# Windowed sums by a scan, conditioning dots placed elsewhere, and weights fetched two ahead, in a two-layer trunk

## The chip, the cores and the metric

One core of a Trainium2 chip runs the whole kernel. Its engines work side by side: TensorE multiplies matrices, VectorE (DVE) and ScalarE (ACT) do elementwise work, GpSimd (POOL) does a little of it and issues some transfers, SyncE (SP) issues most transfers. Each engine takes its instructions in order, and so does each queue of transfers: an instruction that waits holds up everything behind it on the same engine. The metric is the device time of one execution in microseconds (us).

## The reference

One sequence of 1024 tokens with 1024 channels goes through two layers, all in float32.

- Conditioning: `silu(c)` times wide matrices gives, for each layer, a shift, a scale and a gate per channel, and a shift and a scale for the keys and values.
- Layer 0: norm, shift and scale, then `u, z = h @ w_in` with 2048 channels each. The channels of `u` are in four groups of 512. In group g a trailing mean over 2, 4, 8 or 16 tokens (fewer at the start) is taken, minus `u` itself. Each group is multiplied with its own 512 x 512 matrix and with a scale per channel, then with `silu(z)`, and the 2048 channels are multiplied with `w_out` (the output product). The gate times that is added to x.
- Keys and values are made from x, then layer 1 is attention in a window of 128 tokens, gated, with an output product of its own, and a last norm follows.

The trailing mean is, in the reference,

```
upper = c_g[:, 1:]                       # running sum over tokens
lower = jnp.pad(c_g, ((0, 0), (w, 0), (0, 0)))[:, 1:S + 1]
outs.append((upper - lower) / count)     # count = min(t + 1, w)
```

## The kernel before

Channels lie on the 128 partitions and the 1024 tokens along the row. Each float32 operand of a product is split in a high and a low part (ScalarE makes the high part, VectorE subtracts it to get the low part), and a product is three passes of TensorE: high times high, high times low, low times high. With 512 tokens per matmul a half of the row, called q, fills one bank of the eight that TensorE writes to.

Layer 0 runs in this order:

1. The start: norm, and group 0's `u` and group matrix, joined to one product ahead of time.
2. The steps of groups 1 to 3, for each group: `U` twice (256 channels of `u` each), then `Z`, `Y`, `Z`, `Y`. `U` and `Z` steps use a scheme with seven products (`pair_products`, line 681) and seven weight tiles, which VectorE and ScalarE make from two fetched tiles (`weight_parts`, line 632). After a `U` step, `pool_split` (line 593) pools each of its two tiles of 128 channels (`pooled`, line 571) and splits the result into p. A `Y` step multiplies the group's p with the group matrix and gates it (`gated`, line 736); the result goes to DRAM (`kept_g`).
3. The output product, sixteen half products `out_half` (line 926) in the list `order`; eight of them are gathered parts (`gather`, line 837, fetched from `kept_g` and split) times one weight tile of `wao`. Half products of the first five column blocks take both halves of the row, 48 matmuls; the last three take only one. The first six (`BESIDE`) stand in a loop of their own, line 940; the others follow at line 961, together with staging jobs (`JOBS`): `S` fetches a weight tile of layer 1, splits it and stores both parts to DRAM, `A` is one dot of the conditioning. Three jobs are always under way.
4. The late chunks: the second halves of the last three blocks, the first norm statistics of layer 1 and its keys and values. Their work is written out with times (`at`, line 1023): the entries are sorted by time, and that is the order on TensorE, ScalarE, VectorE and GpSimd.

The conditioning is done by VectorE. One column of shift, scale or gate for 128 channels is one dot of a fetched 128 x 1024 tile with `silu(c)` (`ada_dot`, line 266). 16 columns are made at the start. The other 48 are in `rest_cols` and are taken one after the other by `ada_step` (line 277), which takes a tile `tmp`, fetches 512 KB into it on SP's queue and does the dot. The tiles `tmp` are a ring of three, 1024 tokens and 16 leading columns of zeros; pooling, gated results, gathered parts, dots and staging jobs all take their tiles from it in the order in which the code asks for them, and a tile is free once its last reader is done.

Who sets the order: in steps 2 and in the first six half products only TensorE's order is written by hand; the order on the other engines is found by the framework's scheduler, which goes by the order in the code and by its own estimates of durations. From the seventh half product on, the order on all five engines is as written; in the late chunks, on all but SP.

The pooling doubles the window with each pass, over the tile with its leading zeros:

```
while s < w:
    nx = tmp()
    nc.vector.tensor_add(out=nx[:, 2 * s - 1:], in0=cur[:, 2 * s - 1:], in1=cur[:, s - 1:PAD + T - s])
    cur, s = nx, 2 * s
```

So a window of 4 takes two passes, of 8 three, of 16 four. Then the first w - 1 tokens are set right and the mean minus `u` is formed.

Weight tiles of the output product: `half_w` (line 889) fetches a tile into `raw` (two of them) and splits it into `wh` and `wl` (two each), one half product ahead of its use.

Of the kernel before, what the change touches and what calls it, by code (L numbers as in the profile page):

```python
# [15 lines left out]
ALU = mybir.AluOpType  # L16
# [4 lines left out]
T = 1024  # L21
# [5 lines left out]
PAD = 16  # L27
# [15 lines left out]

LATE = 5

ADA = (0, 0, 2, 6, 8, 8)

BESIDE = 6

# [37 lines left out]
def trunk(ctx, tc, xT, c, pack, ada_first, ada_rest, wu0_in, wg0_in, wa, wg, wao, wkv,  # L87
          wb, wbo, bias_in, fg_row, outT, out_last):
    nc = tc.nc
# [61 lines left out]
    def split_w(raw):  # L151
        wh = wp.tile([P, 1024], F32R, tag="wh", name="wh")
        nc.scalar.copy(out=wh, in_=raw)
        wl = wp.tile([P, 1024], F32R, tag="wl", name="wl")
        nc.vector.tensor_sub(out=wl, in0=raw, in1=wh.bitcast(F32))  # L155
        return wh, wl

    def fetch(*srcs):
        r = []
        for src in srcs:  # L160
            r.append(wp.tile([P, 1024], F32, tag="raw", name="raw"))
            nc.sync.dma_start(r[-1], src)
        return r
# [80 lines left out]
    with ExitStack() as sa:  # L244
        ap = sa.enter_context(tc.tile_pool(name="apool", bufs=1))

        def tmp():
            return ap.tile([P, 2 * PAD + T], F32, tag="tmp", name="tmp", bufs=3)[:, :PAD + T]
# [26 lines left out]
        rest_at = [0]  # L275
# [295 lines left out]
        def pooled(g, u):  # L571
            w = WINDOWS[g]
            cur, s = u, 1
            while s < w:
                nx = tmp()
                nc.vector.tensor_add(out=nx[:, 2 * s - 1:], in0=cur[:, 2 * s - 1:],  # L576
                                     in1=cur[:, s - 1:PAD + T - s])
                cur, s = nx, 2 * s
            fix = ap.tile([P, 16], F32, tag="fix", name="fix", bufs=2)
            nc.vector.tensor_mul(out=fix[:, :w - 1], in0=cur[:, PAD:PAD + w - 1],  # L580
                                 in1=rcnt[:, :w - 1])
            out = cur[:, PAD:]
            nc.vector.scalar_tensor_tensor(
                out=out, in0=cur[:, PAD:], scalar=1.0 / w, in1=u[:, PAD:],
                op0=ALU.mult, op1=ALU.subtract)
            nc.vector.tensor_sub(out=out[:, :w - 1], in0=fix[:, :w - 1],
                                 in1=u[:, PAD:PAD + w - 1])
            return out
# [200 lines left out]
        with ExitStack() as after:  # L789
            for ins in last:  # L790
                after.enter_context(tc.issue_after(ins))
            with tc.manual_schedule(engines={ET.PE, ET.Activation, ET.DVE, ET.Pool}):
                w = split_w(*first_raw)
# [6 lines left out]
                w = load_w(wa[17])  # L800
# [54 lines left out]
        with tc.manual_schedule(engines={ET.PE}):  # L855
            nxt = w_first
            for i, (kind, g, j) in enumerate(steps):
                w, nxt = nxt, pair_w(*steps[i + 1]) if i + 1 < len(steps) else None
                if kind == "U":
                    parts = []  # L860
                    pair_products(w, lambda *args: parts.append(args))
                    for t in (1, 0):
                        u = shifted()
                        for tt, q, ps, more in parts:
                            if tt == t:
                                take_u(u, q, ps, more)
                        pool_split(g, 2 * j + t, u)
                elif kind == "Z":
                    gate_tiles[0] = sz = sz_tile()
                    pair_products(w, lambda t, q, ps, more: take_z(sz[:, t, :], q, ps, more))  # L870
                    for d in ((2, 3) if g == 0 else ()):
                        gate_first(d)
                    for _ in range(5 * j if 0 < g < 3 else 0):
                        ada_step()
                    if (g, j) == (3, 1):
                        gather(0, 1, 2, 3)
                else:
                    for t in range(2):

                        ps = gemm_full(w, t * 512, lambda k, hl, q: moving(pts[k][:, hl, half(q)]),  # L880
                                       [0, 1, 3, 2])
                        gf = gated(4 * g + 2 * j + t, (ps, None), gate_tiles[0][:, t, :])
                        if (g, j) == (3, 1):
                            split_g(14 + t, [gf[:, half(q)] for q in range(2)])
                    for _ in range(2 if g < 3 else 0):
                        ada_step()


            def half_w(n, hf):
                return load_w(wao[n, hf])  # L890

            def g_acts(hf):
                return lambda k, hl, q: moving(g_parts[8 * hf + k, q][hl])

            order = ([(0, 0), (1, 0), (0, 1), (1, 1)]
                     + [(n, hf) for n in range(2, KT) for hf in range(2)])
            ws, outs = {}, {}
            staged = [1, 8, 9, 2, 3, 10, 11]

            def ask():  # L900

                if not jobs:
                    return
                raw = tmp()[:, :1024]
                kind = jobs.pop(0)
                if kind == "A":
                    i = rest_at[0]
                    nc.gpsimd.dma_start(raw, ada_rest[i])
                    rest_at[0] += 1
                    asked.append(lambda: ada_dot(raw, cact, *rest_cols[i]))  # L910
                else:
                    i = staged.pop(0)
                    nc.gpsimd.dma_start(raw, wb[i])
                    asked.append(lambda: stage_split(i, raw))

            def stage_split(i, raw):

                hi = stage_hi[i % 2].rearrange("p a c -> p (a c)")
                nc.scalar.copy(out=hi, in_=raw)
                lo = raw.bitcast(F32R)  # L920
                nc.vector.tensor_sub(out=lo, in0=raw, in1=hi.bitcast(F32))
                keep(("b", i), hi, lo, nc.gpsimd)

            ws[0, 0] = half_w(0, 0)
            gather(4, 5, 6, 7)
            def out_half(i):

                n, hf = order[i]
                qs = (0, 1) if n < LATE else (0,)
                if hf == 0:  # L930
                    outs[n] = [next_bank() for _ in qs]
                passes([(q, outs[n][q]) for q in qs], ws[n, hf], 0, g_acts(hf), KT,
                       hf == 0, hf == 1)
                if hf == 1:
                    for q in qs:
                        residual(n, q, outs[n][q], 16)
                    for q in qs:
                        square_add(n, q)

            for i in range(BESIDE):  # L940
                ws[order[i + 1]] = half_w(*order[i + 1])
                if i == 0:
                    gather(8, 9)
                    new_x()
                    again_x(0)
                    gather(10, 11, 12, 13)
                else:
                    again_x(i)
                for _ in range(ADA[i]):
                    ada_step()  # L950
                out_half(i)
# [2 lines left out]

        with tc.manual_schedule(engines={ET.PE, ET.Activation, ET.DVE, ET.Pool, ET.SP}):
            stage_hi = [slot("stage") for _ in range(2)]
            raw = fetch(wao[order[BESIDE + 1]])
            jobs, asked = list("".join(JOBS)), []
            for _ in range(3):
                ask()  # L960
            for i in range(BESIDE, len(order)):
                if i + 1 < len(order):
                    ws[order[i + 1]] = split_w(*raw)
                if i + 2 < len(order):
                    raw = fetch(wao[order[i + 2]])
                if i < KT:
                    again_x(i)
                for _ in JOBS[i - BESIDE]:
                    asked.pop(0)()
                    ask()  # L970
                out_half(i)
            assert rest_at[0] == len(rest_cols) and not staged
            mod_scale(8, 56, C_KVG)
            mod_scale(16, 32, C_NG + 8)

# [47 lines left out]
        def at(t, f, *args):  # L1023
            plan.append((t, len(plan), f, args))

        def put(k, f, *args):
            got[k] = f(*args)
# [31 lines left out]
        for i in range(nl):  # L1059
            at(NT * i, last_chunk, i)  # L1060
            if i % 4 == 3:
                t, n = NT * (i + 1), late[i // 4]
                at(t + AFTER[0], lambda n: residual(n, 1, got[n], 16), n)
                at(t + AFTER[1], square_s, n, 1)
                at(t + AFTER[2], square_a, n, 1)
        at(NT - 0.01, lambda: put("st", rstd_stats, sqh[0], 4))
        at(2 * NT - 0.01, lambda: nc.scalar.copy(out=rb, in_=rstd_spread(got["st"], 4)))
        for i in range(16):
# [939 lines left out]
```

## Time and profile before

| | us |
|---|---|
| three runs | 960.07, 954.99, 959.39 |
| median | 959.39 |
| the profiled execution | 953.02 |
| its span, first to last instruction | 951.3 |
| TensorE busy in it | 916.2 |
| VectorE busy in it | 775.9 |
| ScalarE busy in it | 456.6 |

The profiled execution is one more run, with the hardware's profiler on; its span is what the rows of the profile add up to. Rows give the engine, the line of the kernel (L240 is line 240; a helper's line stands for all its callers), the operation and its tiles (out<-in). In rows with a `|` there follow the busy time in all and the mean in ns, and then the time in which the engine stood idle just before, with what ended it. Rows of the timeline begin with the start and the duration in us; what stands in brackets is the idle time before and what ended it. TensorE's matmuls overlap, so that one lasts 0.38 us and the next begins 0.216 us later.

Places in time: groups 1 to 3 last until about 413 us, the output product from there to 556 us, the late chunks to about 590 us, then keys, values and layer 1.

### The profile page before, as it was taken

To read this page: it belongs to the slowest core of one execution; us is meant where nothing else is said; L and a number is where in the kernel's file an instruction comes from. 1 tells how busy PE (TensorE), PEld (TensorE's weight loads), DVE (VectorE), ACT (ScalarE), POOL (GpSimd) and SP (SyncE) were. 2 spreads that over 40 slices of the span, in tenths; PEclk is the share of its full clock that TensorE was granted. 3 is DMA by queue.
4 is the path that set the end of the run, shared out by engine and by line. 5 is a ranking of instruction groups with operands and counts; after the bars stand their busy time and mean duration, and the time that the engine had idled before them with its cause. 6 is when DMAs were issued, how large, how long until landed. Compare 5 with 4: busy or idle time off the path is not lost.

```text
span 951.3 us, 12686 instructions
## 1 busy us (share of the span) xinstructions
PE 916.2 (96%) x4468; PEld 796.9 (84%) x4468; DVE 775.9 (82%) x1414; ACT 456.6 (48%) x872; POOL 151.0 (16%) x229
## 2 busy tenths in 40 slices
PE   9999899999999998999989999899999999999997
PEld 7787788788888887888768887788888888888897
DVE  6999989777997799776774659579999966879786
ACT  6546554433443344662122335456766444556534
POOL 3000000000000000000012200223213343435621
PEclk9999999999999999999999999999999999999999
DMA  9453451174116420768888843953665744447112
GB/s 348 180 183 111 134 177 66 45 244 155 58 54 243 155 67 23 250 229 304 291 285 296 301 144 120 324 175 125 233 228 191 244 155 156 143 168 179 43 68 110
DMA packets 52081, 166.57 MB, mean 175 GB/s; under 512 B 6705, under 2 KB 7857, under 8 KB 51890
## 3 DMA queue, kind: packets, MB, share of 16 engines
q1 hardware_dynamic: 39346, 119.63, 36.1%
q0 software_dynamic: 12240, 44.57, 14.1%
q10 hardware_dynamic: 432, 1.57, 0.5%
q8 instruction: 35, 0.57, 0.2%
q14 instruction: 28, 0.23, 0.1%
HBM read 129.04 MB, written 36.70 MB: 174 GB/s over the span
## 4 chain that ended last, share of the span: by engine, by line
PE 51%; DVE 30%; DMA 8%; issue 6%; ACT 5%; SPq 0%; DVEq 0%; ACTq 0%; POOLq 0%; POOL 0%
PE ps_d L1255 7%; PE ps_d L1253 7%; PE ps_d L1254 7%; PE ps_d L678 5%; PE ps_d L240 5%; PE ps_S L240 4%; DMA tmp<-ada_rest 3%; DVE tmp L576 3%; PE ps_S L678 2%; DVE ws L649 2%; PE ps_tp L240 2%; DVE ad L267 2%; PE ps_tp L678 2%; DVE wl L155 1%; DVE tw L653 1%
## 5 line engine op out<-in xcount | busy, mean ns | idle before, releaser
L267 DVE CUSTOM_DVE_ANT_0 tmp<-tmp,cact,pk 128x1024 f32<-128x1024 f32 x48 | 60.8, 1284 | 36.3 <-DMA tmp<-ada_rest 36.1
L240 PE MATMUL ps_d<-gh,wh 128*128 128x512 f32 x224 | 79.7, 379 | 0.0
L678 PE MATMUL ps_d<-hs,ws 128*128 128x512 f32 x312 | 72.1, 380 | 1.4 <-ACT ws L648 1.0
L1406 ACT ACTIVATE P<-P,nm 128x129 f32<-128x129 f32 x128 | 50.0, 393 | 42.3 <-DVE nm L1402 40.9
L678 PEld LDWEIGHTS ps_d<-hs,ws 128*128 128x128 f32 x312 | 58.7, 189 | 10.8 <-ACT ws L648 1.4
L1253 PE MATMUL ps_d<-hm,wh 128*128 128x512 f32 x176 | 67.4, 383 | 0.0
L1254 PE MATMUL ps_d<-hm,wh 128*128 128x512 f32 x176 | 66.7, 379 | 0.0
L1255 PE MATMUL ps_d<-hm,wl 128*128 128x512 f32 x176 | 66.7, 379 | 0.0
L240 PE MATMUL ps_S<-gh,wh 128*128 128x512 f32 x192 | 65.1, 380 | 0.0
L648 ACT CAST ws<-tw 128x512 fp32r<-128x512 f32 x52 | 31.9, 619 | 59.8 <-DVE tw L653 30.8
L678 PE MATMUL ps_d<-ha,ws 128*128 128x512 f32 x252 | 57.8, 379 | 0.0
L678 PEld LDWEIGHTS ps_d<-ha,ws 128*128 128x128 f32 x252 | 47.6, 189 | 6.8
L568 POOL MEMSET tmp<- 128x16 f32 x12 | 1.3, 111 | 327.2 <-DVE tmp L576 112.3
L240 PEld LDWEIGHTS ps_d<-gh,wh 128*128 128x128 f32 x224 | 42.3, 189 | 6.0
L576 DVE TENSOR_TENSOR tmp<-tmp 128x1039 f32<-128x1039 f32 (+3 forms) x36 | 44.4, 1234 | 1.0
L1439 POOL TENSOR_SCALAR_AFFINE_SELECT pp<-ph 128x1024 fp32r<-128x1024 f32 x28 | 32.9, 1176 | 60.5 <-DVE ph L1431 60.4
L240 PE MATMUL ps_d<-gh,wl 128*128 128x512 f32 x112 | 42.4, 379 | 0.0
L240 PEld LDWEIGHTS ps_S<-gh,wh 128*128 128x128 f32 x192 | 36.1, 189 | 5.0
L240 PE MATMUL ps_d<-p,wh 128*128 128x512 f32 x96 | 36.6, 381 | 2.4 <-ACT p L598 1.7
L1471 DVE SCALAR_TENSOR_TENSOR of<-ps_o,ol 64x256 f32<-64x256 f32 x64 | 26.6, 415 | 14.6 <-ACT ol L1465 13.8
L1255 PE MATMUL ps_d<-hm,raw 128*128 128x512 f32 x96 | 36.5, 380 | 1.9 <-DMA raw<-kw 1.9
L678 PE MATMUL ps_S<-hs,ws 128*128 128x512 f32 x156 | 36.3, 381 | 1.5 <-ACT ws L648 1.5
(354 smaller groups left out, 2654.8 us busy)
## 6 DMA issues: line engine op xcount, KB each, us to landing
tmp<-ada_rest SPq DMA_DIRECT2D x42, 512.0 KB, 4.4
raw<-wa SPq DMA_DIRECT2D x28, 512.0 KB, 3.4
raw<-wao SPq DMA_DIRECT2D x20, 512.0 KB, 5.7
raw<-kw POOLq DMA_DIRECT2D x20, 512.0 KB, 4.4
wh<-kw POOLq DMA_DIRECT2D x19, 512.0 KB, 3.6
wl<-kw POOLq DMA_DIRECT2D x19, 512.0 KB, 4.5
ad<-ada_first SPq DMA_DIRECT2D x16, 512.0 KB, 5.1
x<-xT SPq DMA_DIRECT2D x32, 256.0 KB, 5.8
```

What stands on the lines that cost most here:

```text
L240: mm(p, lhs, acts(k, hl, q), start=start and k == ks[0] and s == 0, stop=stop and k == ks[-1] and s == 2)
L267: nc.vector.tensor_tensor_reduce(out=raw, in0=raw, in1=ca, scale=0.5, scalar=pk[:, bcol:bcol + 1], op0=ALU.mult, op1=ALU.add, accum_out=ad ...
L576: nc.vector.tensor_add(out=nx[:, 2 * s - 1:], in0=cur[:, 2 * s - 1:], in1=cur[:, s - 1:PAD + T - s])
L648: nc.scalar.copy(out=ws[i][:, 0, :], in_=src)
L649: nc.vector.tensor_sub(out=ws[i][:, 1, :], in0=src, in1=ws[i][:, 0, :].bitcast(F32))
L678: mm(ps, lhs, acts(k, hl), start=start and k == 0 and s == 0, stop=k == 3 and s == 2, skip_group_check=True)
L1253: mm(p, lh, a[0](), start=k == 0, stop=False)
L1254: mm(p, lh, a[1](), start=False, stop=False)
L1255: mm(p, ll, a[0](), start=False, stop=k == n - 1)
L1406: note(ACT, 0.41, lambda: nc.scalar.activation(pt()[:, i, :P + 1], pt()[:, i, :P + 1], AF.Exp, bias=nm()[:, i:i + 1], scale=-1.0, accum_ou ...
L1439: note(POOL, 1.12, lambda: nc.gpsimd.affine_select(out=v8(prev()), in_=v8(cur()).bitcast(F32), pattern=[[0, 8], [-1, 2], [-2, P // 2]], ba ...
L1471: note(DVE, 0.36, lambda: nc.vector.scalar_tensor_tensor(out=of()[e * 64:(e + 1) * 64, :], in0=o()[0:64, es], scalar=0.5, in1=ol()[0:64, e ...
```

## The change

Three things change.

- `pooled`: for windows of 8 and 16 one scan instruction takes the place of the passes. It keeps a running value along the row: add `u[t]`, subtract `u[t - w]`. One tile `tmp` is taken for it, where 3 or 4 were.
- The dots of the conditioning are placed otherwise. Groups 1, 2, 3 have 5, 6, 3 dots at a `Z` step (the second one in groups 1 and 2, the first one in group 3; before 5, 5, 0), and 2, 4, 3 at a `Y` step (in groups 1 and 2 after each of the two, in group 3 after the first one; before 2, 2, 0). The first six half products have 0, 0, 1, 2, 3, 3 where they had 0, 0, 2, 6, 8, 8. The six `A` jobs stay. What is left of the 48 is written into the late chunks, at 0.4 us and then every 1.5 us.
- In the first six half products a weight tile is fetched two half products ahead and split one ahead, where both stood one ahead. The later ones had this already.

```diff
-ADA = (0, 0, 2, 6, 8, 8)
+ADA = (0, 0, 1, 2, 3, 3)
+
+ADA_Z, ADA_Y = (0, 5, 6, 3), (0, 2, 4, 3)
...
         def pooled(g, u):
             w = WINDOWS[g]
             cur, s = u, 1
+            if w > 4:
+                cur, s = tmp(), w
+                nc.vector.tensor_tensor_scan(cur[:, PAD:], u[:, PAD:], u[:, PAD - w:PAD + T - w],
+                                             0.0, op0=ALU.add, op1=ALU.subtract)
             while s < w:
...
-                    for _ in range(5 * j if 0 < g < 3 else 0):
+                    for _ in range(ADA_Z[g] if j == (g < 3) else 0):
                         ada_step()
...
-                    for _ in range(2 if g < 3 else 0):
+                    for _ in range(ADA_Y[g] if g < 3 or j == 0 else 0):
                         ada_step()
...
+            raw = fetch(wao[order[1]])
             for i in range(BESIDE):
-                ws[order[i + 1]] = half_w(*order[i + 1])
+                ws[order[i + 1]] = split_w(*raw)
+                raw = fetch(wao[order[i + 2]])
...
-            raw = fetch(wao[order[BESIDE + 1]])
...
-            assert rest_at[0] == len(rest_cols) and not staged
+            assert not staged
...
+        n_late = len(rest_cols) - rest_at[0]
+        for i in range(n_late):
+            at(0.4 + 1.5 * i, ada_step)
```

## The prediction

> **What bounds the kernel now.** I read the page's first part, then TensorE's waits stage by stage, then the rows of what those waits wait for.
>
> ```profile
> span 951.3 us, 12686 instructions
> ...
> PE 916.2 (96%) x4468; PEld 796.9 (84%) x4468; DVE 775.9 (82%) x1414; ACT 456.6 (48%) x872; POOL 151.0 (16%) x229
> ...
> PEclk9999999999999999999999999999999999999999
> ```
>
> TensorE is busy 916.2 of 951.3 us at a granted clock of 0.9 or more in every slice, and the change takes no matmul away. So what can be won is part of the 35.1 us in which TensorE stands still. The waits of TensorE in groups 2 and 3 (270 to 400 us), and then in the output product (410 to 560 us; columns: total, times, longest):
>
> ```profile
> PE ps_d L240 <- ACT p L598: 1.7, 1, 1.7
> PE ps_o L678 <- ACT ps_o L689: 1.1, 1, 1.1
> PE ps_d L240 <- DVE p L599: 0.6, 1, 0.6
> PE ps_o L678 <- ACT ps_d L689: 0.3, 1, 0.3
> ```
>
> ```profile
> PE ps_o L240 <- DVE wl L155: 4.4, 2, 2.4
> PE ps_tp L240 <- DVE wl L155: 2.1, 2, 1.1
> PE ps_S L240 <- DVE wl L155: 0.4, 1, 0.4
> ```
>
> These are 3.7 us and 6.9 us, 10.6 us in all: the ceiling of the two stages that the change touches. In the output product TensorE waits each time for wl, the low half of a weight tile, which VectorE makes. VectorE isn't short of time there; it stands in line. The stages (busy us of TensorE, weight loads, VectorE, ScalarE, GpSimd; then clock, DMA share, GB/s), VectorE's scale-column dots from 415 to 560 us, and one of the five waits in time:
>
> ```profile
> 222.10:384.90 162.80, 159.06 (x734) 137.84 (x733) 144.33 (x201) 68.70 (x109) 0.89 (x8) 1.00 0.31 107
> 384.90:413.40 28.50, 28.50 (x134) 24.96 (x133) 20.43 (x27) 18.67 (x27) 0.00 (x0) 1.00 0.72 249
> 413.40:454.70 41.30, 41.30 (x193) 36.18 (x192) 29.67 (x41) 18.23 (x22) 0.00 (x0) 1.00 0.83 292
> 454.70:502.60 47.90, 41.36 (x189) 34.96 (x188) 35.19 (x51) 9.42 (x12) 2.92 (x5) 1.00 0.84 291
> 502.60:556.30 53.70, 53.30 (x247) 46.36 (x246) 28.96 (x34) 15.62 (x18) 11.85 (x22) 1.00 0.84 293
> ```
>
> ```profile
> L267 DVE CUSTOM_DVE_ANT_0 tmp<-tmp,cact,pk 128x1024 f32<-128x1024 f32 x30 | 37.9, 1287 | 30.7 <-DMA tmp<-ada_rest 30.7
> ```
>
> ```profile
> 451.26 1.28 DVE L267 CUSTOM_DVE_ANT_0 tmp<-tmp,cact,pk 128x1024 f32<-128x1024 f32 x1 [3.02 <-DMA tmp<-ada_rest]
> 453.09 1.28 DVE L267 CUSTOM_DVE_ANT_0 tmp<-tmp,cact,pk 128x1024 f32<-128x1024 f32 x1 [0.54 <-DMA tmp<-ada_rest]
> 454.96 0.74 DVE L728 SCALAR_TENSOR_TENSOR x<-ps_d,adac,x 128x512 f32<-128x512 f32 x1
> 455.62 1.21 DVE L155 TENSOR_TENSOR wl<-raw,wh 128x1024 fp32r<-128x1024 f32 x1
> ```
>
> ```profile
> 456.89 0.48 PE L240 MATMUL ps_tp<-gh,wl 128*128 128x512 f32 x1 [1.07 <-DVE wl L155]
> ...
> 530.74 0.48 PE L240 MATMUL ps_S<-gh,wl 128*128 128x512 f32 x1 [0.40 <-DVE wl L155]
> ```
>
> A dot of 1.28 us waits 3.02 us for its 512 KB while the DMA engines are 0.83 busy; the residual and then wl stand behind it; TensorE needs wl at 455.8 and goes on at 456.9. So the output product is held up by transfers, through VectorE's order. In groups 2 and 3 the DMA engines are 0.31 busy, but VectorE is 144.3 of 162.8 us.
>
> **The change part by part.**
>
> *A. Dots leave the output product.* Of the 24 dots in its first six half products 9 stay (0, 0, 1, 2, 3, 3 where 0, 0, 2, 6, 8, 8 stood). 15 dots are 15 x 0.524 = 7.9 MB; at the 291 GB/s above that is 27 us of transfer, and the dots waited 30.7 us for transfers. What was last in line, wl, then waits for no dot of a late transfer. I take away 6.5 of the 6.9 us and leave the 0.4 us, which falls at 530.7, in the staging part, whose jobs stay as they were. Bounds: all 6.9; or, if the other transfers keep the engines full (502.6 to 556.3 runs at 0.84 too, with few dots), only 2.
>
> *B. The scan.* For windows of 8 and 16 it takes the place of 3 and 4 passes of L576, for eight tiles:
>
> ```profile
> L576 DVE TENSOR_TENSOR tmp<-tmp 128x1039 f32<-128x1039 f32 (+3 forms) x28 | 34.5, 1232 | 0.7
> ...
> L267 DVE CUSTOM_DVE_ANT_0 tmp<-tmp,cact,pk 128x1024 f32<-128x1024 f32 x11 | 13.9, 1280 | 3.1 <-DMA tmp<-ada_rest 3.1
> ```
>
> The 28 passes of 222 to 385 us go: 34.5 us. No scan is in this trace. Lower end: the dot of L267, 1.28 us, which also does two steps per element over 1024 and carries a sum along. Upper end: the four passes that it replaces, 4 x 1.232 = 4.93 us. I take 1.28, the nearest row: eight scans are 10.2 us, and VectorE gains 24.3 us.
>
> [...]
>
> What the gain is worth is read at the pooled tiles. The last p of group 3 ends two chains of four passes in a row; with a scan each they are 2 x (4.93 - 1.28) = 7.3 us shorter, more than the 1.7 + 0.6 us that TensorE waits for that p. Those 2.4 us go. The other two waits, 1.1 and 0.3 us, are for seeds that ScalarE copies behind weight parts that VectorE makes between pooling passes; I take away 0.5 of their 1.4. B: -2.9 us, bounds -3.7 and 0.
>
> *D. Dots arrive in groups 2 and 3.* Group 2 has 14 where it had 9, group 3 has 6 where it had none: 11 more. One costs VectorE (13.9 + 3.1) / 11 = 1.55 us with its wait in this stage, so 17.0 us, fewer than the 24.3 freed. Their 11 transfers are 5.8 MB over 162.8 us, 35 GB/s on top of 107. They go through SP's queue, each behind a free tmp (ring of three), and fetches of weights (raw<-wa, raw<-wg), stores of kept_g and the gathers stand behind them. Weights are made one step ahead, and a U or Z step lasts 18 us (seven products of 2.59, the first row below), so a few us late on SP is covered; without the cover, two dots more after Y(2,1) are 3.1 us on the path. I take 0, bounds 0 and +3.1.
>
> ```profile
> 319.41 2.59 PE ps_d L678 x12
> ```
>
> ```profile
> 431.57 1.64 DVE L835 TENSOR_TENSOR gh<-gr,gh 128x512 fp32r<-128x512 f32 x2
> ```
>
> *E. Fetch two ahead.* The same SP issues, each one half earlier. None of TensorE's waits above ends with raw<-wao, so it is worth 0 by itself. If the earlier transfers push the gathers, one 0.524 MB at 292 GB/s is 1.8 us; the last gathered part is split at 433 us (second row above), and TensorE, which begins the second halves near 434, uses it five of eight steps later.
>
> *C. Four dots come late.* 14 + 15 + 9 + 6 = 44 of 48 dots; four are written into the next stage at 0.4, 1.9, 3.4 and 4.9 us, in VectorE's written order. Before v, the statistics of the norm, stand the first two.
>
> ```profile
> 559.88 0.16 DVE L191 TENSOR_SCALAR v<-ps_o 128x4 f32<-128x4 f32 x1 [1.09 <-PE ps_o L188]
> 564.14 0.75 DVE L1000 SCALAR_TENSOR_TENSOR tmp<-x,acol,rb 128x512 f32<-128x512 f32 x1 [4.09 <-ACT rb L1067]
> ```
>
> ```profile
> 551.30 0.53 POOL L174 DMA_DIRECT2D kw<-tmp  x1 [0.91 <-DVE tmp L921]
> 560.13 1.03 POOL L193 TENSOR_TENSOR rs<-v,mhalf 128x4 f32<-128x4 f32 x1 [8.31 <-DVE v L191]
> ```
>
> ```profile
> kw<-tmp POOLq DMA_DIRECT2D x1, 512.0 KB, 6.9
> ```
>
> ```profile
> DMA to landing us min/median/max: 3.3/4.1/5.1
> ```
>
> ```profile
> 562.38 1.05 PE L200 MATMUL ps_tp<-ident,rs 128*128 128x128 f32 x8
> ```
>
> The thirteen staging jobs take the three tmp in turn, so the second late dot gets the tmp of the twelfth job, whose store to DRAM is issued at 551.30 and lands 6.9 us later, at 558.2. The transfer of the dot then takes 3.3 us at best (the landing of these transfers in group 2, last row but one): 561.5; the dot ends at 562.8, and v comes at 562.8, not at 559.88: +2.9 us. From v to the end of rs it is 1.28 us (560.13 + 1.03 - 559.88), so rs is there at 564.1, and TensorE, which comes to the spread (L200) at 562.38, waits about 1.7; with the median landing it would be 2.5. I take 2.0. VectorE's next work (L1000) shifts by the same and then runs without a hole, so nothing gives it back. Dots three and four fall into the 4.09 us in which VectorE waits for rb anyway. Bounds: 0 (the transfers early enough) and +3.5 (landing in 5.1 us).
>
> **The sum.** -6.5 - 2.9 + 0 + 0 + 2.0 = -7.4 us. The profiled execution took 953.02 us (span 951.3, 1.7 around it), so its like would be 945.6. The runs shown have a median of 959.39, 6.4 above it; I put the difference on that: **952.0 us**.
>
> **The rivals.**
>
> [...]
>
> *2. The waits move.* The order on VectorE and SP in the groups is the scheduler's, by its own durations; dots whose transfers are late stand ahead of the pooling and the weight parts as they now stand ahead of wl. For it: 3.1 us of such waits by 11 dots already. Against: the DMA engines are 0.31 busy there. B is lost and D costs 3.1: -6.5 + 2.0 + 3.1 = -1.4, 958.0.
>
> *3. The output product isn't relieved.* Gathers, x and staging keep the engines at 0.84, A is 2 us: -2 - 2.9 + 2.0 = -2.9, 956.5. For it: the share of 502.6 to 556.3. Against: TensorE waited only 0.4 us there.
>
> *4. Slower: VectorE becomes the bound in groups 2 and 3.* With a scan of S us it needs 144.3 - 34.5 + 17.0 + 8 S of 162.8 us; it is full at S = 4.5, from where each us of S adds 8, and B is gone. A less C is 4.5 us, so the kernel is slower from S = 5.1, just above the upper end. At S = 6: 8 x 1.5 - 4.5 = +7.5, 966.9. For it: each element needs the sum before it. Against: the dot carries a sum at 1.28 us.
>
> **How the numbers follow.** Chances: forecast 0.38, half rate 0.22, waits move 0.20, not relieved 0.12, slower 0.08. About 0.5%, 4.8 us, is what a measurement can tell from no change. The forecast and the half rate lie 2 to 3 us beyond that bound and land inside it about one time in four; the second and third rival mostly lie inside. Faster 0.55, same 0.35, slower 0.10. The range goes from the profiled execution's like (945.6) down to 945, since A, B at their ends (-6.9 - 3.7) with C at 0 give 948.8 on the median, and up to 960: the scan at 4.93 us (8 S is 3.4 us over what is free: -6.5 + 2.0 + 3.4 = -1.1) with C at its end (1.5 more) gives 959.8.
>
> **What would show it.** Right: no wait of TensorE for wl over 0.5 us before 500 us; VectorE's wait for ada_rest in the output product down from 30.7 us to under 12; eight L576 passes left and eight scans under 2.5 us; no wait for the last p; a new wait of some 2 us at the spread, with v behind a late dot. Wrong: waits for seeds, p or weight parts growing in the groups, a scan over 4.5 us, or waits for wl that stay with fewer dots.

## The result, and the profile after

| | before | after |
|---|---|---|
| median of 20 runs each (us) | 956.8 (952.06 to 960.07) | 959.15 (956.17 to 966.91) |
| ratio to before | 1 | 1.0044, 95% interval 1.0027 to 1.0060 |
| span of the profiled execution (us) | 951.3 | 955.4 |
| mean granted clock in it | 0.996 | 0.994 |

The forecast was 952.0 us, faster. The changed kernel is slower by 0.44%, less than the 0.5% that was named as the bound of "no change", but the interval excludes 1. With more runs the median of before came out at 956.8, 2.6 below the median of the three runs that the forecast started from; so against its own base the forecast said -7.4 us, and it became +2.35.

The changed kernel's page, the first lines and the group of the dots and of the scan (busy us, mean ns, then the idle time just before):

```profile
span 955.4 us, 12660 instructions
...
PE 917.9 (96%) x4468; PEld 799.0 (84%) x4468; DVE 760.4 (80%) x1394; ACT 456.2 (48%) x872; POOL 150.9 (16%) x229
...
L269 DVE CUSTOM_DVE_ANT_0 tmp<-tmp,cact,pk 128x1024 f32<-128x1024 f32 x48 | 60.9, 1282 | 27.7 <-DMA tmp<-ada_rest 27.5
```

```profile
L578 DVE TENSOR_TENSOR_SCAN tmp<-tmp 128x1024 f32<-128x1024 f32 x8 | 18.3, 2288 | 0.5
```

VectorE did lose work: 760.4 us busy where it was 775.9. Of the 4.1 us more of span, TensorE is busy for 1.7 (917.9 against 916.2, with the same matmuls) and idle for 2.4. TensorE's waits in the changed kernel, first from 222 to 420 us (groups 2 and 3), then from 420 to 640 us (us in all, times, longest):

```profile
PE ps_S L684 <- ACT ps_S L695: 4.9, 2, 3.6
PE ps_d L684 <- ACT ps_S L695: 1.3, 1, 1.3
PE ps_o L684 <- ACT ps_S L695: 1.2, 1, 1.2
PE ps_d L684 <- ACT ps_d L695: 0.8, 2, 0.5
PE ps_o L684 <- ACT ps_d L695: 0.8, 1, 0.8
PE ps_S L684 <- ACT ps_d L695: 0.4, 1, 0.4
```

```profile
PE ps_d L1265 <- DMA raw<-kw: 2.4, 1, 2.4
PE ps_tp L242 <- DVE wl L157: 2.3, 1, 2.3
```

Groups 2 and 3 wait 9.4 us in all where they waited 3.7. No wait for p is left; every wait is for a seed, the copy that ScalarE makes (L695) to start a product of `pair_products`. In the output product the five waits for wl, 6.9 us, are gone until 550 us, and one of 2.3 us has come at its end, at 553.71 us.

The largest wait, followed back. VectorE of the changed kernel in time (start and duration in us; in brackets the idle time before and its releaser), the four dots behind the second `Y` step of group 2 and the first weight part after them:

```profile
324.53 1.28 DVE L269 CUSTOM_DVE_ANT_0 tmp<-tmp,cact,pk 128x1024 f32<-128x1024 f32 x1 [1.25 <-DMA tmp<-ada_rest]
...
328.13 1.28 DVE L269 CUSTOM_DVE_ANT_0 tmp<-tmp,cact,pk 128x1024 f32<-128x1024 f32 x1 [2.30 <-DMA tmp<-ada_rest]
...
332.14 1.28 DVE L269 CUSTOM_DVE_ANT_0 tmp<-tmp,cact,pk 128x1024 f32<-128x1024 f32 x1 [2.71 <-DMA tmp<-ada_rest]
...
333.35 1.28 DVE L269 CUSTOM_DVE_ANT_0 tmp<-tmp,cact,pk 128x1024 f32<-128x1024 f32 x1
...
334.55 0.68 DVE L659 TENSOR_TENSOR tw<-raw 128x512 f32<-128x512 f32 x1
```

SP's queue at that place, the time from issue to landing of its last row (the weight tile), then ScalarE and TensorE:

```profile
322.71 0.33 SPq L750 DMA_DIRECT2D kept_g<-tmp  x1
323.09 0.42 SPq L283 DMA_DIRECT2D tmp<-ada_rest  x1
...
325.86 0.80 SPq L283 DMA_DIRECT2D tmp<-ada_rest  x2
326.75 0.38 SPq L164 DMA_DIRECT2D raw<-wa  x1
```

```profile
DMA to landing us min/median/max: 7.7/7.7/7.7
```

```profile
335.33 0.62 ACT L654 CAST ws<-tw 128x512 fp32r<-128x512 f32 x1 [9.62 <-DVE tw L659]
335.85 0.58 ACT L695 COPY ps_S<-ps_tp 128x512 f32<-128x512 f32 x1
```

```profile
336.48 4.54 PE L684 MATMUL ps_S<-ha,ws 128*128 128x512 f32 x12 [3.62 <-ACT ps_S L695]
340.86 2.75 PE L684 MATMUL ps_d<-ha,ws 128*128 128x512 f32 x12
```

SP issues the transfers of three of the four dots only from 323.09 us on, behind a store of `kept_g`; the third dot's at 325.86, when the first dot has freed its tile, and the fourth's right behind it. VectorE stands 1.25 + 2.30 + 2.71 = 6.3 us for the dots' tiles. The weight part at 334.55 is behind the dots; ScalarE has stood idle for 9.62 us before it casts the result; the seed is behind the cast; TensorE, which ran out of work at 332.86, waits 3.62 us for the seed.

There is a second way to the same moment. That weight part reads the second weight tile of its step, and SP issues its fetch at 326.75, behind the dots' transfers. It lands 7.7 us later, at about 334.5; the tile fetched before it (issued at 317.67) took 3.2. So the tile is there and VectorE is free within 0.1 us of each other, and by these rows either one alone would have held TensorE up by about as much.

Afterwards twelve matmuls take 4.54 us, where twelve take 2.75 in the next row. Two stretches of the changed kernel (busy us of TensorE, weight loads, VectorE, ScalarE, GpSimd, then the granted clock, the DMA share and GB/s):

```profile
325.00:332.00 7.00, 7.00 (x34) 6.15 (x33) 2.12 (x4) 0.57 (x1) 0.11 (x1) 1.00 0.86 297
337.20:340.62 3.42, 3.42 (x9) 2.67 (x9) 3.42 (x7) 2.92 (x6) 0.00 (x0) 0.50 0.28 98
```

The stage average of 0.31 that the prediction used hid this: between 325 and 332 us the DMA engines are 0.86 busy at 297 GB/s. That is 2.1 MB, about the size of the three dots' tiles and the one weight tile that SP issues one after the other there. And the granted clock is 0.50 for 3.4 us after the wait, so another 4.54 - 2.75 = 1.8 us are lost.

The other new wait, at the end of the output product (VectorE, then TensorE):

```profile
551.22 1.28 DVE L269 CUSTOM_DVE_ANT_0 tmp<-tmp,cact,pk 128x1024 f32<-128x1024 f32 x1 [3.25 <-DMA tmp<-ada_rest]
...
552.43 1.22 DVE L157 TENSOR_TENSOR wl<-raw,wh 128x1024 fp32r<-128x1024 f32 x1
...
562.13 0.16 DVE L193 TENSOR_SCALAR v<-ps_o 128x4 f32<-128x4 f32 x1 [1.08 <-PE ps_o L190]
562.25 1.28 DVE L269 CUSTOM_DVE_ANT_0 tmp<-tmp,cact,pk 128x1024 f32<-128x1024 f32 x1
```

```profile
553.71 0.48 PE L242 MATMUL ps_tp<-gh,wl 128*128 128x512 f32 x1 [2.31 <-DVE wl L157]
```

A late dot stands ahead of the last wl of the part before, waits 3.25 us for its transfer, and TensorE waits 2.31 us for that wl. The statistics v are not held up; they wait for TensorE.

Where the 4.1 us arise is seen when the n-th matmul of after is set beside the n-th of before (both traces have 4468). At the start of group 2 after is 0.6 us ahead (before has 3.4 us at a clock of 0.50 from 33.0 us on, after hasn't). At the end of group 3 it is 8.0 us late, just before the last wl 0.3 early, just after it 2.3 late, after the wait for raw near 614 us 4.2 late, and at the end 4.1 late. So groups 2 and 3 cost 8.5 us, of which the lists above show 5.7 more of waits and 1.8 of clock. The output product gives back 8.3 (6.9 of waits), the last wl takes 2.6 (2.31 of wait), and the wait for raw takes 1.9: it is 0.5 longer (2.37 against 1.88), and the clock is 0.50 again from 613.7 to 617.1 us. A wait takes some 0.26 us more than its idle time, as I estimate from the rows: the overlap of two matmuls is lost (0.38 less 0.216), and the first one behind the wait lasts 0.48 and not 0.38. This makes up most of the differences.

### The profile page after: what moved, and what is told of

Read it like the earlier page. It is cut to its first block, busy times and chain, and to the rows that moved or that the text cites. A ratio compares the mean times of both kernels' runs of the same rounds, so it can differ in the third digit from the quotient of the medians.

```text
span 955.4 us, 12660 instructions
## 1 busy us (share of the span) xinstructions
PE 917.9 (96%) x4468; PEld 799.0 (84%) x4468; DVE 760.4 (80%) x1394; ACT 456.2 (48%) x872; POOL 150.9 (16%) x229
## 4 chain that ended last, share of the span: by engine, by line
PE 55%; DVE 27%; DMA 7%; issue 5%; ACT 4%; DVEq 0%; SPq 0%; POOL 0%; ACTq 0%; POOLq 0%
PE ps_d L242 8%; PE ps_d L1265 7%; PE ps_d L1263 7%; PE ps_d L1264 7%; PE ps_S L242 5%; PE ps_d L684 5%; PE ps_S L684 3%; PE ps_tp L242 3%; PE ps_o L242 2%; DMA tmp<-ada_rest 2%; DVE tmp L578 2%; DVE ad L269 2%; DVE ws L655 2%; DMA raw<-wa 2%; DVE tw L659 1%
## 5 line engine op out<-in xcount | busy, mean ns | idle before, releaser
L155 ACT CAST wh<-raw 128x1024 fp32r<-128x1024 f32 x24 | 25.4, 1060 | 47.0 <-PE ps_d L242 28.9
L157 DVE TENSOR_TENSOR wl<-raw,wh 128x1024 fp32r<-128x1024 f32 x24 | 29.3, 1222 | 19.4 <-ACT wh L155 17.7
L1412 DVE CUSTOM_DVE_ANT_0 P<-ps_S,bias,nsink 128x128 f32<-128x128 f32 x128 | 37.5, 345 | 0.2
```

The lines of the kernel that those rows point to most:

```text
L1412: note(DVE, 0.28, lambda: nc.vector.tensor_tensor_reduce(out=pt()[:, i, :P], in0=s()[:, e, :P], in1=bias[:, hd, :], scale=-1.0, scalar=nsi ...
```

## The experiments

Two theories after the result. **Q (a queue):** dots whose transfers come late stand ahead of weight parts on VectorE, ScalarE's seeds stand behind these, and TensorE waits; how full VectorE is doesn't matter. **S (the scan):** the scan, 2.288 us each, fills VectorE, or blocks it, and this makes the waits of the groups. Ratios are to the kernel before, run on the same chip beside it; waits of TensorE are those of one profiled execution.

**The scan alone.** The kernel before with

```diff
             cur, s = u, 1
+            if w > 4:
+                cur, s = tmp(), w
+                nc.vector.tensor_tensor_scan(cur[:, PAD:], u[:, PAD:], u[:, PAD - w:PAD + T - w],
+                                             0.0, op0=ALU.add, op1=ALU.subtract)
             while s < w:
```

> The kernel before with the scan alone. Theory Q (queue: what costs the time in groups 2 and 3 is the dots whose transfers VectorE waits for, with the weight parts and then ScalarE's seeds behind them): the scan by itself is a gain. It takes 2.29 us (measured in the changed kernel) for 3 or 4 passes of 1.23, 16.2 us of VectorE in all; TensorE's waits for p (2.4 us) go and the seeds' waits (1.4 us) shrink: 2 to 4 us faster, the waits in the output product stay at about 7 us. Theory S (the scan at half rate fills VectorE at the wrong moments): seeds wait longer in group 2 and 3 with the scan alone too, 3 us or more, and the kernel is no faster than before.

Measured: 953.16 us, ratio 0.9999 (0.9975 to 1.0022). TensorE's waits in groups 2 and 3:

```profile
PE ps_d L682 <- ACT ps_S L693: 1.3, 1, 1.3
PE ps_d L682 <- ACT ps_tp L693: 1.3, 1, 1.3
PE ps_S L682 <- ACT ps_d L693: 0.4, 1, 0.4
PE ps_o L682 <- ACT ps_d L693: 0.4, 1, 0.4
```

The 2.4 us of waits for p are gone as forecast, but seeds cost 3.4 us where they cost 1.4: 3.4 in all against 3.7. VectorE and ScalarE of this kernel just before the first of them (TensorE goes on at 254.16):

```profile
245.33 2.29 DVE L576 TENSOR_TENSOR_SCAN tmp<-tmp 128x1024 f32<-128x1024 f32 x1
247.54 1.58 DVE L603 TENSOR_TENSOR p<-tmp,p 128x1024 fp32r<-128x1024 f32 x1
...
249.05 0.74 DVE L657 TENSOR_TENSOR tw<-raw 128x512 f32<-128x512 f32 x1
```

```profile
249.90 0.62 ACT L652 CAST ws<-tw 128x512 fp32r<-128x512 f32 x1 [2.05 <-DVE tw L657]
251.64 1.46 ACT L602 CAST p<-tmp 128x1024 fp32r<-128x1024 f32 x1 [1.12 <-DVE tmp L590]
...
253.52 0.58 ACT L693 COPY ps_S<-ps_d 128x512 f32<-128x512 f32 x1
```

The scan and the work on p are one stretch on VectorE, with no weight part between; the weight part comes at 249.05, and the cast of p then stands ahead of the seed on ScalarE. So the scan moves work among VectorE's and ScalarE's places without moving the end. Q had expected a gain of 2 to 4 us here, and it did not come; what S said of this run (seeds 3 us or more, no faster) did.

**The dots alone.** The changed kernel without the scan and without the fetch two ahead:

```diff
-            if w > 4:
-                cur, s = tmp(), w
-                nc.vector.tensor_tensor_scan(...)
...
-                ws[order[i + 1]] = split_w(*raw)
-                raw = fetch(wao[order[i + 2]])
+                ws[order[i + 1]] = half_w(*order[i + 1])
```

> The changed kernel without the scan (passes as before) and without the earlier fetch: only the dots are moved. Theory Q: the wait of 3.6 us before group 3's first U ends and the slower clock behind it are there as in the changed kernel, and VectorE has 16.2 us less to spare, so TensorE's waits in groups 2 and 3 are 10 us or more: 2 to 8 us slower than the changed kernel. Theory S: without the scan the long wait goes, and this is faster than the changed kernel by 2 us or more.

Measured: 963.17 us, ratio 1.0080 (1.0051 to 1.0110), the slowest of all. Groups 2 and 3 wait 8.7 us; the wait at the end of the output product is 5.3 us:

```profile
PE ps_d L242 <- ACT p L600: 3.8, 1, 3.8
...
PE ps_tp L242 <- DVE wl L157: 5.3, 1, 5.3
```

So the slowdown comes with the dots and needs no scan: S falls as its cause. Q's number was too high (10 us or more in the groups), and the wait of 3.6 us before group 3's first U, which Q expected here too, is 1.2, with the same four dots ahead of it:

```profile
334.21 1.13 PE L680 MATMUL ps_S<-ha,ws 128*128 128x512 f32 x4 [1.23 <-ACT ps_S L691]
```

With the scan alone TensorE doesn't wait there at all. So, as far as single executions show it, that longest wait takes the dots and the order that VectorE has with the scan together; in that one point S was right. In this placement p is late (3.8 us), which the scan cures.

**Four fewer dots in group 2.** The changed kernel with two dots at each `Y` of group 2, and four more in the output product:

```diff
-ADA = (0, 0, 1, 2, 3, 3)
+ADA = (0, 0, 2, 4, 4, 3)
-ADA_Z, ADA_Y = (0, 5, 6, 3), (0, 2, 4, 3)
+ADA_Z, ADA_Y = (0, 5, 6, 3), (0, 2, 2, 3)
```

> The changed kernel with two dots, not four, after each Y of group 2; the four are put back into the output product (0, 0, 2, 4, 4, 3). Theory Q: VectorE's three waits for transfers at 323 to 332 us (6.3 us) fall to one or two of together 2 us, TensorE's wait of 3.6 us and the stretch at the lower clock behind it (1.8 us) go: 5 us faster than the changed kernel, some 2 to 3 us faster than the kernel before; the output product stays free of waits or gets 1 us of them. Theory S: the wait in group 3 stays above 2 us, and the time is within 1 us of the changed kernel's.

Measured: 956.06 us, ratio 1.0012 (0.9990 to 1.0035), 0.3% below the changed kernel's, where Q expected 5 us, and no faster than before. Groups 2 and 3 wait 4.3 us; the wait of 3.6 us near 336 is gone, as Q said; the longest in these groups is 1.3. But the output product, where Q expected 1 us at most, has 6.5: two waits for wl of 1.2 us are back, with thirteen dots in the first six half products, and the late one is 4.1:

```profile
PE ps_tp L242 <- DVE wl L157: 6.5, 3, 4.1
```

**No late dots.** The changed kernel, with the four late dots put into the output product:

```diff
-ADA = (0, 0, 1, 2, 3, 3)
+ADA = (0, 0, 2, 3, 4, 4)
```

> The changed kernel with no dot in the late chunks; the four are put back into the output product (0, 0, 2, 3, 4, 4). Groups 2 and 3 are untouched. If the first late dot costs what the trace shows (TensorE waits 2.3 us for wl, which stands behind the dot's transfer), that wait goes and the kernel is 2 to 3 us faster than the changed kernel. If the shorter wait for raw<-kw (2.4 against 1.9 us) and the lower clock at 602 to 628 us come from it too, it is 3.5 to 4 us. If the late dots cost nothing by themselves, under 1 us.

Measured: 954.30 us, ratio 0.9997 (0.9981 to 1.0013), 0.47% below the changed kernel's. No wait for a wl of the output product is left, neither within it nor at its end, although thirteen dots stand in its first six half products. Groups 2 and 3 still wait 9.1 us. The wait at the seed of group 3 is 1.0 us shorter, though nothing was changed there, and the clock doesn't fall behind it (1.00 from 333 to 341 us):

```profile
335.57 2.86 PE L684 MATMUL ps_S<-ha,ws 128*128 128x512 f32 x12 [2.63 <-ACT ps_S L695]
```

**The same dots without transfers.** The changed kernel, with the four dots behind the second `Y` of group 2 reading a tile that is there already. Four conditioning columns then hold something else, so what follows from them is not the reference's; number and length of VectorE's instructions stay.

```diff
-                        ada_step()
+                        if (g, j) == (2, 1):
+                            nc.vector.tensor_tensor_reduce(out=tmp()[:, :T], in0=cact, in1=cact, ...)
+                        else:
+                            ada_step()
```

> The changed kernel in which the four dots after the second Y of group 2 read a tile that already lies there instead of a fetched one: the same work on VectorE, the same tiles taken from the ring, no transfer. Four columns of the conditioning hold something else for it, so the output isn't the reference's. Theory Q, in the form that it is the transfers: VectorE's three waits (6.3 us) and TensorE's wait of 3.6 us go with them, under 1.5 us is left there, and the lower clock after it too; 3 to 5 us faster than the changed kernel. If it is VectorE's own time (four dots of 1.28 us ahead of the weight parts), TensorE still waits 2.5 us or more at this place and the time is within 2 us of the changed kernel's.

Measured: 954.59 us, ratio 1.0017 (0.9992 to 1.0042). The dots, and the weight part behind them:

```profile
323.95 1.27 DVE L893 CUSTOM_DVE_ANT_0 tmp<-cact,pk 128x1024 f32<-128x1024 f32 x1
...
329.37 0.68 DVE L659 TENSOR_TENSOR tw<-raw 128x512 f32<-128x512 f32 x1
```

The four run one behind the other in 5 us, and the weight part comes at 329.37 and not at 334.55. TensorE doesn't wait for the product that stood 3.62 us; three products later it waits 0.8. The clock doesn't drop there (that product's twelve matmuls, from 334.14, take 2.75 us). By the two ratios this is some 2.6 us less than the changed kernel, where 3 to 5 were expected, and their intervals overlap. With the same work on VectorE, the wait is that of the transfers: that part of Q is shown. Which way it takes isn't, since SP's queue is relieved as well. It now issues the second weight tile ahead of the last store, 10.8 us before TensorE comes to the product at 334.14; in the changed kernel it was 6.1 us before (326.75 to 332.86):

```profile
323.39 0.33 SPq L164 DMA_DIRECT2D raw<-wa  x1
```

**Both placements mended.** The changed kernel with two dots at each `Y` of group 2 and none late:

```diff
-ADA = (0, 0, 1, 2, 3, 3)
+ADA = (0, 0, 3, 4, 5, 5)
-ADA_Z, ADA_Y = (0, 5, 6, 3), (0, 2, 4, 3)
+ADA_Z, ADA_Y = (0, 5, 6, 3), (0, 2, 2, 3)
```

> Two dots instead of four after each Y of group 2, and no late dots; eight more in the output product (0, 0, 3, 4, 5, 5). If the two causes add up, groups 2 and 3 have TensorE's waits of the run with four fewer (4.4 us), the late chunks none for wl, and the output product 0 to 3 us of waits with 17 dots where 24 made 6.9: 4 to 7 us faster than the changed kernel, 0 to 3 us faster than the kernel before. If 17 dots are again too many for the output product (4 us of waits or more), it is as fast as the kernel before.

Measured: 950.53 us, ratio 0.9956 (0.9934 to 0.9977): faster than both kernels. The gain over the kernel before, 0.44%, is a little more than the 0 to 3 us expected. Groups 2 and 3 wait 4.6 us, and with seventeen dots in the first six half products there is still no wait for a wl there. So in this placement it was enough for the 6.9 us to take away seven of the 24 dots of before, not fifteen. The number isn't all: thirteen dots left 2.4 us in the run with four fewer and none in the run without late dots, and the runs don't show why.

**The fetch alone.** The kernel before with weights fetched two ahead:

```diff
+            raw = fetch(wao[order[1]])
             for i in range(BESIDE):
-                ws[order[i + 1]] = half_w(*order[i + 1])
+                ws[order[i + 1]] = split_w(*raw)
+                raw = fetch(wao[order[i + 2]])
```

> The kernel before with the earlier fetch alone: all 24 dots stay in the output product. If the fetch by itself is worth nothing, TensorE's five waits for wl there stay at 5 to 7 us and the time is within 1.5 us of the kernel before. If it is the earlier weight tile that removed them in the changed kernel, they fall under 2 us and the kernel is 5 us faster.

Measured: 954.36 us, ratio 1.0012 (0.9988 to 1.0037). The waits for wl in the output product stay, 5.8 us where they were 6.9:

```profile
PE ps_o L240 <- DVE wl L155: 3.9, 2, 2.1
PE ps_tp L240 <- DVE wl L155: 1.9, 2, 1.5
```

**Three late dots, behind v.** Two dots at each `Y` of group 2, five at its `Z`, and the three that are left written at 2.6 us, behind the statistics:

```diff
-ADA = (0, 0, 1, 2, 3, 3)
+ADA = (0, 0, 2, 4, 4, 5)
-ADA_Z, ADA_Y = (0, 5, 6, 3), (0, 2, 4, 3)
+ADA_Z, ADA_Y = (0, 5, 5, 3), (0, 2, 2, 3)
...
-            at(0.4 + 1.5 * i, ada_step)
+            at(2.6 + 0.1 * i, ada_step)
```

> The changed kernel with the dots elsewhere: groups 1 and 2 as before (5 and 2, 2), 3 and 3 in group 3, 15 in the output product (0, 0, 2, 4, 4, 5), and three late ones written behind v, where VectorE waits for rb anyway. Expected from the waits of the runs so far: no wait for wl in the staging part (the late dots can't stand ahead of it), none at the spread, 1 to 2.5 us in the output product, 4 to 5 us in groups 2 and 3: 3 to 5 us faster than the kernel before. If late dots cost wherever they stand, TensorE's wait at the spread or the keys grows by 2 us and it is no faster than before.

Measured: 950.32 us, ratio 0.9955 (0.9931 to 0.9979). The late dots cost no wait at all behind v; TensorE's only wait for a wl of the output product is 0.4 us, and the groups wait 5.9.

**That placement with the passes.** The last kernel without the scan:

```diff
-            if w > 4:
-                cur, s = tmp(), w
-                nc.vector.tensor_tensor_scan(...)
```

> The placement of the eighth run (dots of group 2 as before, six in group 3, three behind v, fewer in the output product, fetch two ahead), with the 28 passes of L576 in place of the eight scans. Theory Q (the queue of dots, weight parts and seeds decides, and VectorE's total does not): the scan's 16.2 us of VectorE are worth nothing here either, as in the first run; groups 2 and 3 wait 5 to 7 us, ratio to the kernel before 0.993 to 0.998. Theory S turned round (the scan makes the room for the six dots of group 3): waits for the last p grow to 5 us or more as in the second run (3.75 us for p at 383), ratio 1.000 to 1.005.

Measured: 951.98 us, ratio 0.9960 (0.9944 to 0.9976), where the scan gave 0.9955. Groups 2 and 3 wait 4.2 us in all; p is waited for again, and there are fewer waits for seeds:

```profile
PE ps_d L242 <- ACT p L600: 1.7, 1, 1.7
PE ps_d L242 <- DVE p L601: 1.1, 1, 1.1
PE ps_o L680 <- ACT ps_o L691: 1.1, 1, 1.1
PE ps_o L680 <- ACT ps_d L691: 0.3, 1, 0.3
```

The 5 us or more that the other side expected for p don't come (2.8). Where the dots stand well, the scan earns nothing that can be measured.

**The scan for the window of 16 only.** The same placement:

```diff
-            if w > 4:
+            if w > 8:
```

> The placement of the eighth run, with the scan only for the window of 16 (group 3, four scans instead of 16 passes); group 2 goes back to its 12 passes of 1.23 us, three of which take 3.7 us in the place of one scan of 2.29. Theory Q: the seed waits of group 2 (1.28 and 0.42 at 349 and 368 in the eighth run), which the block of the scan brought, shrink to those of before (1.1 and 0.3), and the waits of group 3 stay; ratio 0.993 to 0.998, no difference to the eighth run that can be measured. If VectorE's total in the groups mattered, 5.6 us more of it there (12 passes of 1.23 less four scans of 2.29) would show as longer waits for p in group 2, ratio over 0.999.

Measured: 949.58 us, ratio 0.9935 (0.9912 to 0.9959), the best of the kernels run. Groups 2 and 3 wait 3.6 us, the least of all kernels that have the dots there. Its intervals overlap with those of the two runs before, so that it beats them isn't shown; that it beats the kernel before and the changed one is. VectorE's waits for dots in groups 2 and 3 are 5.0 us in its profiled execution, and 11.4 in the changed kernel's. The seed waits follow the scan. In group 2, which has the passes again, the two of 1.2 and 0.4 us that the scan had made there (near 254 and 273 us in the run with three late dots behind v) are gone, and the one of 1.1 us near 275 is back as before. The waits of 1.3 and 0.4 that the expectation put into group 2 (349 and 368 us) lie in group 3, where the scan stays, and they stay too.

## Why the prediction was wrong, point by point

**A, dots leave the output product (-6.5): right.** All 6.9 us of waits for wl went, in the place named. They went without the earlier fetch too (the dots alone), and stayed with the fetch alone. The bound from below (other transfers keep the engines full, only 2) did not come true; seventeen dots, and thirteen in one of two placements, left none either. What was not seen is that part of the move was for nothing, and that the dots had to be put somewhere worse.

**B, the scan (-2.9): mis-sized, and the step behind it failed.** The scan takes 2.288 us, not the 1.28 of the dot that I took as the nearest row; two of the passes that it replaces, 2 x 1.232 = 2.46, were nearer. No run before the forecast had a scan in it, so neither a scan as long as the dot nor the "half rate" that has a chance of 0.22 was shown by any; the changed kernel showed 2.288 us, 1.86 times a pass. By an estimate from these rows this length alone would have cost little: two chains of four passes become 2 x (4.93 - 2.288) = 5.3 us shorter and not 7.3, still more than the 2.3 us that TensorE waited for that p. What failed is "Those 2.4 us go": the waits for p went, and 2.0 us of waits for seeds came in their place, by the run with the scan alone, because the scan and the work on p leave no gap for a weight part; group 2 got its old waits back when it got its passes back (the scan for the window of 16 only). By waits B is -0.3, and by time nothing that can be measured, in two placements (0.9999 against 1; 0.9955 against 0.9960).

**D, dots arrive in the groups (0, bounds 0 and +3.1): the step that failed most.** It failed at "so a few us late on SP is covered". The weight tile that was needed next went out at 326.75, behind the dots' transfers, and landed at 334.5, when TensorE had been without work since 332.9: the cover was used up. VectorE stood in line at the four dots till the same moment, and this the prediction had priced with an average, 1.55 us a dot with its wait and two dots more, 3.1. The four together waited 6.3 us, since three transfers begin late, held up by SP's order and by the ring of tiles, and share the engines. A DMA share of 0.31 over 163 us said nothing of the 7 us at 0.86. Against the run with the scan alone D cost 6.0 us of waits (9.4 less 3.4) and 1.8 of clock. That the transfers make this wait is shown (the same dots without transfers); how much of it goes through VectorE's order and how much through SP's stays open.

The mechanism is that of the second rival, "the waits move", which named both orders. That its 958.0 us lies only 1.2 below the time measured is luck: it had given D at 3.1 as well, it said 1.4 us faster than before where 2.35 slower was measured, and its base of 959.39 was 2.6 too high.

**E, fetch two ahead (0): right.** 1.0012 (0.9988 to 1.0037) alone.

**C, four late dots (+2.0): the size was near, the way was wrong.** The wait came at the last wl, 2.31 us, not at the spread, and v was not behind a dot that waited. I worked with the order written inside the late part and put its first entry behind everything of the part before. In the trace the first late dot is ahead of that part's last wl, so the written order doesn't hold between two parts. Taking all four away made the kernel faster by 0.47% (the ratios 0.9997 and 1.0044), about 4.5 us, more than the 2.3 of this wait; the two profiles also differ at the seed of group 3 (1.0 us of wait and the lower clock) and in the wait for raw near 614 us, so I don't put all 4.5 on the wait. Written behind v, three dots cost nothing, which the prediction had right for its dots three and four.

**The sum.** In place of -6.5 - 2.9 + 0 + 0 + 2.0 the two traces, matmul beside matmul, give -8.3 for A, +8.5 for B and D together, +2.6 for C, +1.9 at the wait for raw and -0.6 before group 2; that these last two come from the change isn't shown. So nearly the whole miss is in B and D, for which -2.9 was forecast. The third and the fourth rival are out: the output product was relieved, and VectorE is less busy than before. Of the signs that the prediction had set, waits for wl, scans under 2.5 us and the wait for the last p came out as for "right"; but waits for seeds in the groups, one of its signs for "wrong", grew from 1.4 to 9.4 us.

**Left open:** profiled executions of one kernel and its neighbours reach the same place up to 2 us apart before any edit has acted (from 17 us on, the scan-alone kernel and the one with three late dots behind v are about 2 us later at the same work than the kernel before), and I found no cause for it. So a single span isn't evidence for 1 or 2 us, and the verdicts above rest on the medians.

## What to carry to other kernels

A dot that is filler work was cheap on the engine here and dear in its queue (1.28 us of VectorE each, but 6.3 us of waits for four of them near 330 us): ask not how busy the engine is, but what stands right behind the instruction that may wait for a transfer and right behind its transfer in the queue, and whether four of them in a row can be fed at that moment. Price such a group by its own few microseconds of DMA share and of free tiles, not by the stage's average, and look for places behind which nothing urgent stands (here behind v: three dots for nothing). When an engine's work is shortened, follow the next-latest wait before counting the gain: here a wait for p became a wait for a seed, and 16 us of VectorE's time were worth nothing that could be measured.

## What the runs showed of the hardware

Some waits of TensorE cost far more than their length, and others of a like length did not. In the changed kernel, after 3.62 us without work the granted clock was 0.50 for 3.4 us, and twelve matmuls took 4.54 us; after 2.63 us at the same place, in the kernel without late dots, they took 2.86, as after the wait of 1.30 at 251 us in the changed kernel. The kernel with the dots alone, which waits 3.8 and 5.3 us, has the lowest mean granted clock of the profiled executions, 0.989 against 0.992 to 0.998 in the others. A slower stretch came after shorter waits too. At the wait for raw near 605 to 620 us the next matmul took 0.79 or 0.80 us after 1.69 (the dots without transfers), 2.06 (the passes) and 2.37 us (the changed kernel), but 0.48 after 1.88 (before) and 2.16 us (the scan alone). The kernel with the passes and the one with the scan alone:

```profile
605.47 0.79 PE L1261 MATMUL ps_d<-hm,raw 128*128 128x512 f32 x1 [2.06 <-DMA raw<-kw]
```

```profile
612.20 0.48 PE L1259 MATMUL ps_d<-hm,raw 128*128 128x512 f32 x1 [2.16 <-DMA raw<-kw]
```

In the kernels with four fewer dots and without late dots the next matmul took 0.48 after 1.15 and 1.89 us, but the clock was 0.50 a little later, from 613.5 to 616.8 and from 610.8 to 614.1. In these runs the length of the wait doesn't tell the outcomes apart, and none of them shows what does.
